# A two-block network with 64 expert evaluations on one core: four shared weight slots, a written-out TensorE order in the expert stage, second norms on transposed copies, and a ten-step root

## The chip, the cores and the metric

The kernel runs on one core of one Trainium2 chip, as one program. The time is the device time of one execution in microseconds. A core has five engines that run their own instruction streams: TensorE (PE, with its weight loads shown as PEld), VectorE (DVE), ScalarE (ACT), GpSimd (POOL) and SyncE (SP), which here issues the DMA transfers. All data are fp32. Where precision matters, a value is split into a high part rounded to the matmul format fp32r and a low part (the rest), and products are summed.

## The reference

The input is 256 tokens of width 1024. Block 1 has two layers, block 2 has two more of another kind, with 16 meta tokens put ahead of the sequence. Both blocks, cut to what matters here:

```python
for i in range(2):                                   # block 1
    mix = retention_diff_mixer(x) if i == 0 else mla_gla_mixer(x)
    x = layer_norm(ALPHA * x + mix, ln1_g[i], ln1_b[i])
    x = layer_norm(ALPHA * x + hier_moe(x), ln2_g[i], ln2_b[i])

def hier_moe(x):            # 4 groups x 8 experts; a token takes 2 experts of its best group
    # weights 1024x512 (gate), 1024x512 (up), 512x1024 (down) for each of 32 experts
    hdn = silu(xb @ w_gate[e]) * (xb @ w_up[e])
    return hdn @ w_down[e]  # then scattered back to the tokens, times the gate weight

def rms_norm(x, g):         # block 2: ahead of each layer's two halves
    return x * rsqrt(mean(x * x) + 1e-6) * g
```

In block 2 a layer is a chunked state-space mixer (SSD) beside a sliding-window attention, and then an MLP.

## The kernel before, in words

`body` (L1871) opens a pool `b1` for block 1, runs `mixer_a` (L364), the first expert stage `moe` (L667), a second norm `norm2` (L1913), `mixer_c` (L994), the second expert stage and the second norm again; it then opens pool `b2` and runs `Block2.layer` (L1435) twice.

**The weight ring.** All large weights come through a ring of slots of 128 x 2048 fp32 (1 MB each), handed out in turn by `wslot` (L144). In the expert stages `moe_ring` (L1881) has 19 entries: W and V 4 each, one S, X 4, five entries that are H tiles, and one more. The H tiles are a rotating set of `NH` = 9 (L32) that serves other data too. In an expert stage the normed tokens take three of them (`xn`, and its parts `xh` and `xl`), and the gathered tokens of four experts take one each time they are gathered, with two in use at a change. A tile is given to its new owner as soon as the last reader of the old one is done, and the load that writes it waits for that. SyncE issues loads strictly in order, so a load that waits holds up those behind it. Up to eight loads are under way at a time: load n waits also for load n-8 to have landed.

**The expert stage.** `moe` first norms the tokens (`ln_norm`, L301), routes them with small VectorE operations, and then goes over 16 pairs of experts (L921 and after). A pair has 128 slots, 64 for each expert, and the two experts' products are packed in the two column halves of TensorE's array. For each pair come twelve 1 MB loads (`load_pair`, L681: gate, up, down, each in two halves for two experts), `gate_up` (L837: 64 matmuls 128x512), on every second pair `gather` for the next four experts (L822: 32 matmuls 128x256 with one-hot matrices), `slots` (L902: two transposes of `m_PG`), `down` (L849: silu on ScalarE and VectorE, four transposes of `t2k`, ScalarE's copy `m_hT`, 32 matmuls), and `scatter` of the pair before (L874: eight matmuls on `m_pgT` and `t4k`, added to the result by VectorE). An overflow loop (L940) runs the experts that got more than 64 tokens. A list scheduler of the framework sets each engine's order from the recorded program, on TensorE too: it interleaves pieces of one pair with those of the next.

**The second norm.** `ln_stats` (L287) takes means and variances by rows, `rsqrt` (L219) takes 1/sqrt in 13 VectorE operations: an integer guess and three Newton steps. `ln_norm` writes the normed rows, half on VectorE and half on ScalarE. `norm2` then multiplies and adds gain and bias, laid out as rows over all partitions (`H<-in_ln_g`, `H<-in_ln_b`), in eight VectorE operations 128x512. After the first expert stage `to_fm` (L262) transposes the result on TensorE, in four groups of four, and `hilo` splits each group: a ScalarE cast for the high part, a VectorE subtraction for the low part. After the second stage TensorE transposes too, and the groups are copied to block 2's `h`; squares of the rows are summed on ScalarE, a small root gives each token's RMS factor, and TensorE spreads it over the partitions (`r1`). The meta tokens have a root of their own (`before_next`). In block 2 `sum_sq` (L1347), `inv_rms` (L1357) and `Block2.rsqrt` (L1366) do the same with ones-matmuls and a root on a wide tile, 128 x 272; `scaled` (L1333) applies it.

Of the kernel before, what the change touches and what calls it, by code (L numbers as in the profile page):

```python
# [125 lines left out]
class K:  # L126
# [92 lines left out]
    def rsqrt(self, v, shape, tag="rsq"):  # L219

        i = self.tl(shape, tag + "_i", 1, I32)
        y = self.tl(shape, tag + "_y", 2)
        t = self.tl(shape, tag + "_t", 1)
        hv = self.tl(shape, tag + "_h", 1)
        self.ts(i, v.bitcast(I32), 1, ALU.logical_shift_right)
        self.ts(y.bitcast(I32), i, -1.0, ALU.mult, float(0x5F3759DF), ALU.add)
        self.ts(hv, v, -0.5, ALU.mult)
# [34 lines left out]
    def to_fm(self, x_tm, f32_out=None, scale=None, bias=None):  # L262

        hi, lo = self.H(F32R), self.H(F32R)
        h = hi[:, : 8 * T].rearrange("p (k t) -> p k t", k=8)
        l = lo[:, : 8 * T].rearrange("p (k t) -> p k t", k=8)
        for j in range(4):
            ps = self.pq()
            for m in range(2):
                for i in range(2):  # L270
                    self.tr(ps[:, (2 * m + i) * P : (2 * m + i + 1) * P], x_tm[:, i, 2 * j + m :: 8])
            v = ps.rearrange("p (k t) -> p k t", k=2)
            self.hilo(h[:, 2 * j : 2 * j + 2], l[:, 2 * j : 2 * j + 2], v)
        return h, l
# [12 lines left out]
    def ln_stats(self, r, n_t=2):  # L287
# [4 lines left out]
        v = self.tl([P, 2], "ln_v", 2)  # L292
# [4 lines left out]
        self.ts(v, mv[:, :, 1], LN_EPS, ALU.add)  # L297
        y = self.rsqrt(v, [P, 2], "lnr")
# [65 lines left out]
def mixer_a(k, x_tm, moe):  # L364
# [134 lines left out]
    k.ts(ss, ss, 1.0 / 128, ALU.mult, EPS, ALU.add)  # L499
    rr = k.rsqrt(ss, [P, 2, 4], "rs8")  # L500
# [8 lines left out]
    gv = k.tl([P, 2, 4], "a_gv", 1)  # L509
# [25 lines left out]
    k.ts(gv, mv[:, :, :, 1], LN_EPS, ALU.add)  # L535
    gr = k.rsqrt(gv, [P, 2, 4], "rs8")
# [130 lines left out]
def moe(k, l, r_in, bufs, gb, rows, csb, lps, lt, then):  # L667
# [181 lines left out]
    def down(ws, g, u, gs):  # L849
# [10 lines left out]
        k.acopy(hT, tp.rearrange("p (q m) -> p q m", q=4))  # L860
        yp = [k.pd(), k.pd()]
# [78 lines left out]
    with k.tc.For_i(0, n_ov, 1) as it:  # L940
# [16 lines left out]
        pgT = k.tl([P, T], "m_pgT", 1)  # L957
# [36 lines left out]
def mixer_c(k, x_tm, xh, xl, moe):  # L994
# [243 lines left out]
    k.ts(s8, s8, 1.0 / 128, ALU.mult, EPS, ALU.add)  # L1238
    r8 = k.rsqrt(s8, [P, 8], "rs8")
# [50 lines left out]
class Block2:  # L1290
    def __init__(self, k, big, prm):

        self.k, self.big, self.prm = k, big, [prm]
# [53 lines left out]
    def sum_sq(self, h, n0, js):  # L1347

        k = self.k
        if js[0] == 0:  # L1350
            self.ss = k.pq()
# [5 lines left out]
    def inv_rms(self, n0):  # L1357

        k, ps = self.k, self.ss
        v = self.tl([P, L2], "r1", 5)  # L1360
        k.ts(v[:, n0:], ps[:, n0:L2], EPS, ALU.add)
        r = self.row()
        self.rsqrt(r[:, n0:], v[:, n0:], [P, L2 - n0])
        return r

    def rsqrt(self, y, v, shape):  # L1366
        k = self.k
        i = self.tl([P, L2], "r1", 5, I32)[: shape[0], : shape[1]]
        t = self.tl([P, L2], "r1", 5)[: shape[0], : shape[1]]
        k.ts(i, v.bitcast(I32), 1, ALU.logical_shift_right)  # L1370
        k.ts(y.bitcast(I32), i, -1.0, ALU.mult, float(0x5F3759DF), ALU.add)
        k.ts(v, v, -0.5, ALU.mult)
        for _ in range(3):
            k.mul(t, y, y)
            k.mul(t, t, v)
            k.stt(y, t, 1.5, y, ALU.add, ALU.mult)
# [58 lines left out]
    def layer(self, l, h, n0, r1=None):  # L1435
# [9 lines left out]
        if r1 is None:  # L1445
            r1 = self.inv_rms(0)
# [424 lines left out]
def body(tc, A, out):  # L1871
    from contextlib import ExitStack

    with ExitStack() as es:
# [3 lines left out]
        with tc.tile_pool(name="b1", bufs=1) as b1:  # L1878
            k.big = b1
            dense_ring = w + [("V", NV, b1, 2048)] * NV  # L1880
            moe_ring = dense_ring + [("S", 1, b1, 2048)] + [("X", NX, b1, 2048)] * NX + [("H", NH, b1, NH_F)] * 5 + [("c_phase", 1, b1, 2048)]  # L1881
# [5 lines left out]
            mt, mr = k.base.tile([P, 8, NM], F32, name="mt"), k.base.tile([NM, 1], F32, name="mr")  # L1887
            prm, rows = {}, {}

            def gain_rows(l):  # L1890

                rows[l] = k.H()[:, :2048].rearrange("p (a d) -> p a d", a=2)
                for a, n in enumerate(("ln2_g", "ln2_b")):
                    k.dma(rows[l][:, a], A[n][l : l + 1].to_broadcast([P, D]))

            def before_next():

                gain_rows(1)
# [6 lines left out]
                v = k.tl([P, 2], "ln_v", 2)[:NM, 0:1]  # L1905
                sq = k.tl([P, 1024], "t4k", NT4)[:NM]
                k.act(sq, r, AF.Square, accum_out=v)
                k.ts(v, v, 1.0 / 1024, ALU.mult, EPS, ALU.add)
                k.acopy(mr, k.rsqrt(v, [NM, 1], "lnr"))
# [3 lines left out]
            def norm2(l, r, stats=None):  # L1913

                xn, x = tm(), tm()
                k.ln_norm(xn, r)
                for c in range(2):
                    s = slice(c * 512, (c + 1) * 512)
                    for i in range(2):
                        k.mul(x[:, i, s], xn[:, i, s], rows[l][:, 0, s])  # L1920
                        k.add(x[:, i, s], x[:, i, s], rows[l][:, 1, s])
                        if stats is not None:
                            sq = k.tl([P, 512], "t2k", NT2)
                            k.act(sq, x[:, i, s], AF.Square, accum_out=stats[:, i, c : c + 1])
                return x
# [25 lines left out]
            r1 = k.pd()
            k.mm(r1[:, 0:NM], mr.to_broadcast([NM, P]), k.ident[:NM, :NM])
            for i in range(2):
                k.mm(r1[:, NM + i * P : NM + (i + 1) * P], rr[:, i : i + 1].to_broadcast([P, P]), k.ident)
        with tc.tile_pool(name="b2", bufs=1) as b2:
# [5 lines left out]
            for j in range(4):  # L1961
# [40 lines left out]
```

## Time and profile before

| | us |
|---|---|
| median of 3 runs | 2601.81 (2600.19 to 2602.08) |
| the profiled execution | 2601.37 |
| its span in the profile | 2599.6 |
| PE busy, of the span | 2422.4 (93%) |
| VectorE busy | 1391.0 (54%) |
| ScalarE busy | 1062.8 (41%) |
| expert stage 1, first gate/up product to last scatter | 174.2 to 641.5 |
| expert stage 2, the same | 854.5 to 1322.0 |
| block 2, from its first dense product | 1347.1 to the end |

Times are in us unless marked ns. In a row of the timeline stand the start, the length, the engine, the line of the code, the operation, what it writes and reads, the tile's shape and how many instructions the row joins; in brackets stands how long the engine had been idle and what it waited for. `SPq` is SyncE's queue of DMA issues: a row's length there is from its first issue to its last, so the time that the queue stands is in it. `pd` and `pq` are PSUM tiles; buffer numbers are left out.

### The profile page before, as it was taken

To read this page: it belongs to the slowest core of one execution; us is meant where nothing else is said; L and a number is where in the kernel's file an instruction comes from. 1 tells how busy PE (TensorE), PEld (TensorE's weight loads), DVE (VectorE), ACT (ScalarE), POOL (GpSimd) and SP (SyncE) were. 2 spreads that over 40 slices of the span, in tenths; PEclk is the share of its full clock that TensorE was granted. 3 is DMA by queue.
4 is the path that set the end of the run, shared out by engine and by line. 5 is a ranking of instruction groups with operands and counts; after the bars stand their busy time and mean duration, and the time that the engine had idled before them with its cause. 6 is when DMAs were issued, how large, how long until landed. Compare 5 with 4: busy or idle time off the path is not lost. (4 is left out here: it accounts for less than half of the span.)

```text
span 2599.6 us, 38742 instructions
## 1 busy us (share of the span) xinstructions
PE 2422.4 (93%) x15405; PEld 1762.8 (68%) x15405; DVE 1391.0 (54%) x2913; ACT 1062.8 (41%) x2134; POOL 8.3 (0%) x23
## 2 busy tenths in 40 slices
PE   8979999999787999999969999999998999999999
PEld 7754333334565433333338988899998898889999
DVE  6862222222576422222258878756556887866654
ACT  3421111110443211111137775655464777564654
POOL 0000000000000000000000000000000000000000
PEclk9989999999889999999979999999999999999999
DMA  8479889999634998999965542345554554335553
GB/s 299 165 296 421 367 348 421 421 402 374 237 130 168 380 385 338 421 421 421 402 223 161 179 137 98 121 162 165 173 177 132 182 173 132 114 119 179 181 187 114
DMA packets 189787, 645.16 MB, mean 248 GB/s; under 512 B 21618, under 2 KB 35988, under 8 KB 139556
## 3 DMA queue, kind: packets, MB, share of 16 engines
q1 hardware_dynamic: 189604, 642.66, 66.0%
q8 instruction: 122, 2.00, 0.3%
q14 instruction: 61, 0.50, 0.1%
HBM read 641.49 MB, written 1.12 MB: 247 GB/s over the span
## 5 line engine op out<-in xcount | busy, mean ns | idle before, releaser
L184 PE MATMUL pd<-U,Y 128*128 128x272 f32 (+1 forms) x7792 | 1011.2, 288 | 15.8 <-ACT U L193 9.2
L184 PEld LDWEIGHTS pd<-U,Y 128*128 128x128 f32 x7792 | 980.6, 189 | 30.7 <-ACT U L193 10.3
L196 DVE TENSOR_TENSOR Y<-w,Y 128x1024 fp32r<-128x1024 f32 x344 | 420.0, 1223 | 262.2 <-ACT Y L193 259.8
L184 PE MATMUL pd<-w,H 128*64 128x512 f32 (+1 forms) x2112 | 502.4, 591 | 0.9 <-DMA w<-in_moe_w_up 0.9
L193 ACT CAST Y<-w 128x1024 fp32r<-128x1024 f32 x344 | 359.7, 1047 | 330.3 <-PE pd L184 287.9
L184 PEld LDWEIGHTS pd<-w,H 128*64 128x64 f32 x2112 | 155.9, 138 | 292.3 <-issue 272.0
L184 PE MATMUL pd<-w,m_hT 128*64 128x512 f32 x1040 | 232.7, 596 | 24.4 <-ACT m_hT L193 24.4
L213 DVE SCALAR_TENSOR_TENSOR t4k<-pd,m_gs,t4k 128x512 fp32r<-128x512 f32 x64 | 48.1, 751 | 272.9 <-ACT t4k L190 270.7
L184 PEld LDWEIGHTS pd<-w,m_hT 128*64 128x64 f32 x1040 | 81.5, 137 | 152.8 <-issue 120.5
L190 ACT ACTIVATE t2k<-pd 128x512 f32<-128x512 f32 (+1 forms) x37 | 21.9, 591 | 296.1 <-PE pd L184 296.1
L190 ACT ACTIVATE t4k<-pd,m_gs 128x512 fp32r<-128x512 f32 x64 | 44.0, 687 | 210.3 <-PE pd L184 193.6
L196 DVE TENSOR_TENSOR t2k<-t2k,pd 128x512 f32<-128x512 f32 (+1 forms) x33 | 22.4, 680 | 178.2 <-PE pd L184 178.2
L196 DVE TENSOR_TENSOR H<-H,pq 128x512 f32<-128x512 f32 x132 | 84.0, 682 | 52.4 <-PE pq L184 52.2
L184 PE MATMUL pd<-Xh,H 128*128 128x512 f32 (+1 forms) x320 | 105.4, 401 | 4.1 <-ACT H L193 4.0
L193 ACT COPY m_hT<-pq 128x512 f32<-128x512 f32 (+1 forms) x34 | 19.5, 573 | 218.4 <-PE pq L187 213.5
L190 ACT ACTIVATE H<-pq,m_gb 128x256 f32<-128x256 f32 (+1 forms) x136 | 64.2, 559 | 99.3 <-PE pq L184 78.8
L213 DVE SCALAR_TENSOR_TENSOR t2k<-t2k,pd 128x512 f32<-128x512 f32 (+1 forms) x33 | 22.4, 678 | 150.6 <-ACT t2k L190 150.6
L213 DVE SCALAR_TENSOR_TENSOR r<-pd,cw,r 128x270 f32<-128x270 f32 (+1 forms) x192 | 87.8, 493 | 3.8 <-ACT r L190 2.3
L184 PEld LDWEIGHTS pq<-m_P,H 128*128 128x128 f32 x544 | 72.8, 206 | 25.0 <-issue 19.5
L184 PEld LDWEIGHTS pq<-t4k,m_pgT 128*128 128x128 f32 x256 | 43.6, 187 | 64.8 <-ACT t4k L190 20.3
L184 PE MATMUL pq<-t4k,m_pgT 128*128 128x512 f32 x256 | 80.1, 426 | 6.3 <-DVE t4k L213 6.3
L193 ACT CAST Xh<-w 128x2048 fp32r<-128x2048 f32 (+4 forms) x34 | 57.3, 1690 | 68.9 <-PE pd L184 54.5
(400 smaller groups left out, 2614.1 us busy)
## 6 DMA issues: line engine op xcount, KB each, us to landing
w<-in_moe_w_gate SPq DMA_DIRECT2D x130, 1024.0 KB, 19.8
w<-in_moe_w_down SPq DMA_DIRECT2D x130, 1024.0 KB, 19.8
w<-in_moe_w_up SPq DMA_DIRECT2D x130, 1024.0 KB, 15.9
w<-in_w_in SPq DMA_DIRECT2D x76, 1024.0 KB, 5.1
w<-in_w_mlp_up SPq DMA_DIRECT2D x32, 1024.0 KB, 5.7
w<-in_w_mlp_down SPq DMA_DIRECT2D x32, 1024.0 KB, 5.0
w<-in_w_ssd_down SPq DMA_DIRECT2D x16, 1024.0 KB, 5.8
w<-in_ev_w_in SPq DMA_DIRECT2D x14, 1024.0 KB, 13.1
```

The source lines that it names most:

```text
L184: return self.nc.tensor.matmul(out, l, r, start=start, stop=stop, **kw)
L190: return self.nc.scalar.activation(out, in_, func, **kw)
L193: return self.nc.scalar.copy(out, in_)
L196: return self.nc.vector.tensor_tensor(out=out, in0=a, in1=b, op=op)
L213: return self.nc.vector.scalar_tensor_tensor(out=out, in0=a, scalar=s, in1=b, op0=op0, op1=op1)
```

## The change

It has four parts.

**Ring.** Four of the ring's entries are H tiles instead of five, so it has 18.

**TensorE's order in the expert stage.** The loop over pairs is put under a manual schedule for TensorE: its instructions stand as the code writes them. `down` is split into `hidden` (silu, transposes, `m_hT`) and `down`, and the loop now writes gate/up, slots, gather on odd pairs, hidden, scatter of the pair before, down. The tile `m_pgT` gets two buffers instead of one. The products themselves, packed in halves, stay.

TensorE in the first expert stage, from the end of one pair's down product into the next pair, before (`w` are weight slots, the tile numbers tell pairs apart):

```order
L184 MATMUL pd_2089<-w_1966,m_hT_2086 64x512
L184 MATMUL pq_2170<-t4k_2106,m_pgT_2021 128x512
L184 MATMUL pq_2170<-t4k_2107,m_pgT_2021 128x512
L184 MATMUL pq_2174<-t4k_2106,m_pgT_2021 128x512
L184 MATMUL pq_2178<-t4k_2106,m_pgT_2021 128x512
L184 MATMUL pd_2136<-w_2112,H_2031 64x512
L184 MATMUL pq_2174<-t4k_2107,m_pgT_2021 128x512
L184 MATMUL pq_2178<-t4k_2107,m_pgT_2021 128x512
L184 MATMUL pq_2182<-t4k_2106,m_pgT_2021 128x512
L184 MATMUL pq_2182<-t4k_2107,m_pgT_2021 128x512
L187 MATMUL pq_2186<-ident,m_PG_2026 128x128 x2
```

Now, the same stage from the end of a pair's gate/up product to its down product:

```order
L184 MATMUL pd_2145<-w_2118,H_2007 64x512
L187 MATMUL pq_2162<-ident,m_PG_2002 128x128 x2
L187 MATMUL pq_2174<-ident,t2k_2170 128x128 x4
L184 MATMUL pq_2181<-t4k_2098,m_pgT_1997 128x512
L184 MATMUL pq_2181<-t4k_2099,m_pgT_1997 128x512
L184 MATMUL pq_2185<-t4k_2098,m_pgT_1997 128x512
L184 MATMUL pq_2185<-t4k_2099,m_pgT_1997 128x512
L184 MATMUL pq_2189<-t4k_2098,m_pgT_1997 128x512
L184 MATMUL pq_2189<-t4k_2099,m_pgT_1997 128x512
L184 MATMUL pq_2193<-t4k_2098,m_pgT_1997 128x512
L184 MATMUL pq_2193<-t4k_2099,m_pgT_1997 128x512
L184 MATMUL pd_2197<-w_2120,m_hT_2179 64x512
```

The scatter (`t4k`, `m_pgT`) has moved from behind its own down product, where single gate/up matmuls of the next pair stood in it, to between the next pair's hidden transposes and its down product.

**Second norms.** Gain and bias are applied to the transposed copies, where a feature is a partition, from a small tile `gc`. After the first stage `to_fm` gets it: ScalarE and VectorE each take half of a group and write it to SBUF, and `hilo` splits that. The token-major `x`, which the next mixer adds at its output, is made by four GpSimd operations 128x1024. After the second stage the gains go into the copies to `h`, the sums of squares come from `sum_sq` for the whole tile, meta tokens included, and `layer` takes `inv_rms` for its first layer too; the row squares, the two small roots and the matmuls for `r1` are gone.

VectorE at the second norm after the first stage, before: the norm (`ln_nb`, `H`), the gains, then the four low parts, read from PSUM (`pq`):

```order
L213 SCALAR_TENSOR_TENSOR ln_nb_3999<-ln_mv_3974,lnr_y_3984 128x2
L210 TENSOR_SCALAR H_3971<-H_135,lnr_y_3984,ln_nb_3999 128x1024
L196 TENSOR_TENSOR H_3972<-H_3971,H_3787 128x512 x2
L196 TENSOR_TENSOR H_3972<-H_3972,H_3787 128x512 x2
L196 TENSOR_TENSOR H_3972<-H_3971,H_3787 128x512 x2
L196 TENSOR_TENSOR H_3972<-H_3972,H_3787 128x512 x2
L196 TENSOR_TENSOR H_4012<-pq_4013,H_4011 128x512
L196 TENSOR_TENSOR H_4012<-pq_4020,H_4011 128x512
```

And now:

```order
L213 SCALAR_TENSOR_TENSOR ln_nb_3990<-ln_mv_3969,lnr_y_3977 128x2
L196 TENSOR_TENSOR Xl_4082<-w_4079,Xh_4081 128x128
L210 TENSOR_SCALAR H_3966<-H_135,lnr_y_3977,ln_nb_3990 128x1024
L210 TENSOR_SCALAR t2k_4001<-pq_3996,gc 128x256
L210 TENSOR_SCALAR t2k_4011<-pq_4006,gc 128x256
L196 TENSOR_TENSOR H_3995<-t2k_4001,H_3994 128x512
L210 TENSOR_SCALAR t2k_4021<-pq_4016,gc 128x256
L196 TENSOR_TENSOR H_3995<-t2k_4011,H_3994 128x512
```

The eight gain operations are gone from VectorE, half-width ones on the transposed groups have come in, and the low parts read two SBUF tiles.

**Root.** `root` takes ten VectorE operations instead of 13, with the small constant added inside; it serves both the narrow and the wide roots.

The diff, cut to its core:

```diff
-    def rsqrt(self, v, shape, tag="rsq"):
+    def rsqrt(self, v, shape, tag="rsq", eps=0.0):
...
-        for _ in range(3):
-            self.mul(t, y, y)
-            self.mul(t, t, hv)
-            self.stt(y, t, 1.5, y, ALU.add, ALU.mult)
+        x = self.tl(shape, tag + "_h", 1)
+        self.root(y, i, t, x, v, eps)
         return y
+    def root(self, y, i, t, x, v, eps):
+        s = 0.703952253
+        g = math.sqrt(s * 0.375)
+        self.ts(x, v, eps, ALU.add)
+        self.ts(i, x.bitcast(I32), 1, ALU.logical_shift_right)
+        self.ts(y.bitcast(I32), i, -1.0, ALU.mult, float(0x5F1FFFF9), ALU.add)
+        self.stt(t, y, -1.0, y, ALU.mult, ALU.mult)
+        self.mul(t, t, x)
+        self.stt(y, t, 2.38924456, y, ALU.add, ALU.mult)
+        self.stt(t, y, s * s * g, y, ALU.mult, ALU.mult)
+        self.mul(t, t, x)
+        self.stt(t, t, -g / 0.3, t, ALU.add, ALU.mult)
+        self.stt(y, t, 5.0 * g * g, y, ALU.add, ALU.mult)
...
-    def to_fm(self, x_tm, f32_out=None, scale=None, bias=None):
+    def to_fm(self, x_tm, gain=None):
...
+            if gain is not None:
+                y = self.tl([P, 512], "t2k", NT2).rearrange("p (k t) -> p k t", k=2)
+                g, b = (gain[:, a, 2 * j : 2 * j + 2] for a in range(2))
+                self.act(y[:, 0], v[:, 0], AF.Identity, scale=g[:, 0:1], bias=b[:, 0:1])
+                self.ts(y[:, 1], v[:, 1], g[:, 1:2], ALU.mult, b[:, 1:2], ALU.add)
+                v = y
             self.hilo(h[:, 2 * j : 2 * j + 2], l[:, 2 * j : 2 * j + 2], v)
...
-        oh, gs = k.tl([P, T], "m_pgT", 1, F32R), k.tl([P, 1], "m_gs", 2)
+        oh, gs = k.tl([P, T], "m_pgT", 2, F32R), k.tl([P, 1], "m_gs", 2)
...
-    for p in range(16):
...
-        g, u = gate_up(ws, xg, o)
-        if prev is not None:
-            scatter(*prev)
-        oh, gs = slots(pg, o)
...
-        prev = (oh, *down(ws, g, u, gs))
-    scatter(*prev)
+    with k.tc.manual_schedule(engines={mybir.EngineType.PE}):
+        for p in range(16):
...
+            g, u = gate_up(ws, xg, o)
+            oh, gs = slots(pg, o)
+            if o and q < 7:
+                pt, pg = hots(q + 1)
+                xg = gathered(pt)
+            hT = hidden(g, u)
+            if prev is not None:
+                scatter(*prev)
+            prev = (oh, *down(ws, hT, gs))
+        scatter(*prev)
...
-            moe_ring = dense_ring + [("S", 1, b1, 2048)] + [("X", NX, b1, 2048)] * NX + [("H", NH, b1, NH_F)] * 5 + [("c_phase", 1, b1, 2048)]
+            moe_ring = dense_ring + [("S", 1, b1, 2048)] + [("X", NX, b1, 2048)] * NX + [("H", NH, b1, NH_F)] * 4 + [("c_phase", 1, b1, 2048)]
...
+            def gains_0():
+                rows.append(k.H()[:, :2048].rearrange("p (a d) -> p a d", a=2))
+                for a, n in enumerate(("ln2_g", "ln2_b")):
+                    k.dma(rows[0][:, a], A[n][0:1].to_broadcast([P, D]))
+                    k.dma(gc[:, 0, a], A[n][0].rearrange("(p k) -> p k", p=P))
...
-            x = norm2(0, r)
-            xh, xl = k.to_fm(x)
+            xn, x = tm(), tm()
+            k.ln_norm(xn, r)
+            xh, xl = k.to_fm(xn, gc[:, 0])
+            for i in range(2):
+                for a, op in enumerate((ALU.mult, ALU.add)):
+                    k.nc.gpsimd.tensor_tensor(out=x[:, i], in0=(x if a else xn)[:, i], in1=rows[0][:, a], op=op)
...
+            for kk in range(8):
+                v = xps[kk // 2][:, kk % 2 * T : kk % 2 * T + T]
+                g, c = gc[:, 1, 0, kk : kk + 1], gc[:, 1, 1, kk : kk + 1]
+                if kk % 2:
+                    k.act(h[:, kk, NM:], v, AF.Identity, scale=g, bias=c)
+                else:
+                    k.ts(h[:, kk, NM:], v, g, ALU.mult, c, ALU.add)
+                b.sum_sq(h, 0, [kk])
+            b.layer(0, h, 0)
```

More of the change, by code (lines that the diff above doesn't have):

```diff
@@ L847, in gate_up, with hidden @@
         return gu
-    def down(ws, g, u, gs):
+    def hidden(g, u):
         th = k.tl([P, 512], "t2k", NT2)
@@ L860, in down @@
         k.acopy(hT, tp.rearrange("p (q m) -> p q m", q=4))
+        return hT
+    def down(ws, hT, gs):
         yp = [k.pd(), k.pd()]
@@ L1350, in sum_sq @@
         if js[0] == 0:
[L1351 removed]
+            self.ss = k.pd() if self.ss is None else k.pq()
         for j in js:
@@ L1359, in inv_rms @@
         k, ps = self.k, self.ss
-        v = self.tl([P, L2], "r1", 5)
-        k.ts(v[:, n0:], ps[:, n0:L2], EPS, ALU.add)
         r = self.row()
-        self.rsqrt(r[:, n0:], v[:, n0:], [P, L2 - n0])
+        self.rsqrt(r[:, n0:], ps[:, n0:L2], [P, L2 - n0])
         return r
     def rsqrt(self, y, v, shape):
[L1367 to L1376, printed above, removed]
+        i, t, x = (self.tl([P, L2], "r1", 5, d)[: shape[0], : shape[1]] for d in (I32, F32, F32))
+        self.k.root(y, i, t, x, v, EPS)
     def dense(self, w, cols, xh, xl, n0, evac, nk=8, pairs=False, whole=False):
@@ L1904, in before_next @@
                 k.acopy(mt, ps[:, 0:128].rearrange("p (k t) -> p k t", k=8))
[L1905 to L1909, printed above, removed]
+                r = k.tl([P, 512], "t2k", NT2)[:16, 0:P]
+                for a, n in enumerate(("ln2_g", "ln2_b")):
+                    k.dma(r[8 * a : 8 * a + 8], A[n][1].rearrange("(k p) -> k p", p=P))
+                ps = k.pq()
+                k.tr(ps[:, 0:16], r)
+                k.acopy(gc[:, 1], ps[:, 0:16].rearrange("p (a k) -> p a k", a=2))
                 w = k.tl([P, 512], "t2k", NT2)
                 prm.update(params(k, 0, k.base, [w[:, 0:P], w[:, P : 2 * P]]))
[L1913 to L1925, printed above, removed]
             k.set_ring(moe_ring)
-            r = moe.run(r, bufs, lambda: gain_rows(0))
+            r = moe.run(r, bufs, gains_0)
             k.set_ring(dense_ring)
-            x = norm2(0, r)
-            xh, xl = k.to_fm(x)
+            xn, x = tm(), tm()
[4 more added lines that the diff above has]
+                    k.nc.gpsimd.tensor_tensor(out=x[:, i], in0=(x if a else xn)[:, i], in1=rows[0][:, a], op=op)
             moe = Moe(k, 1)
@@ L1947, in body @@
                         kk = 2 * j + m
-                        k.tr(ps[:, (2 * m + i) * P : (2 * m + i + 1) * P], x[:, i, kk * P : (kk + 1) * P])
+                        k.tr(ps[:, (2 * m + i) * P : (2 * m + i + 1) * P], xn[:, i, kk * P : (kk + 1) * P])
                 xps.append(ps)
[L1951 to L1954, printed above, removed]
         with tc.tile_pool(name="b2", bufs=1) as b2:
```

69 lines of the change are left out of this document (21 added, 48 removed).

## The prediction

> **What bounds the kernel now.** I read the table by stage first (where time is spent, whether TensorE or the transfers fill it), then the DMA queue's waits and SyncE's rows (why the transfers pause), then TensorE's rows. Windows: start and end, length, busy time of PE, PEld, DVE, ACT, POOL, then granted clock, DMA share, GB/s.
>
> ```profile
> 262.00:278.00 16.00, 14.40 (x69) 6.32 (x68) 2.14 (x4) 4.07 (x8) 0.00 (x0) 1.00 0.63 245
> 320.00:340.00 20.00, 18.40 (x90) 7.78 (x91) 2.13 (x4) 4.84 (x10) 0.00 (x0) 1.00 0.38 144
> 340.00:560.00 220.00, 207.12 (x921) 83.74 (x918) 51.74 (x92) 30.85 (x54) 0.00 (x0) 1.00 1.01 422
> 560.00:580.00 20.00, 18.40 (x90) 7.78 (x91) 1.37 (x2) 4.83 (x10) 0.00 (x0) 1.00 0.89 360
> 930.00:960.00 30.00, 28.40 (x130) 12.16 (x127) 7.64 (x14) 6.26 (x12) 0.00 (x0) 1.00 0.84 342
> 1000.00:1022.00 22.00, 20.40 (x99) 8.57 (x100) 2.13 (x4) 4.83 (x10) 0.00 (x0) 1.00 0.44 172
> 1240.00:1260.00 20.00, 18.40 (x91) 7.94 (x92) 1.37 (x2) 4.83 (x10) 0.00 (x0) 1.00 0.88 355
> ```
>
> In both expert stages the transfers run at 422 GB/s, and a load of 1,024 KB takes 2.485 us, the 12 loads of a pair of experts 29.8 us. There are three holes a stage. Each is worth its length times the missing part of 422: 6.7 + 13.2 + 2.9 = 22.8 us in the first stage, 5.7 + 13.0 + 3.2 = 21.9 in the second. In each hole SyncE's queue stands before one load, which issues as TensorE ends the gate and up product of an odd pair (267.04 + 7.08 = 274.12, and 323.75 + 10.51 = 334.26; the third is alike):
>
> ```profile
> 274.18 0.33 SPq L181 DMA_DIRECT2D w<-in_moe_w_up  x1
> 334.64 0.33 SPq L181 DMA_DIRECT2D w<-in_moe_w_gate  x1
> 267.04 7.08 PE L184 MATMUL pd<-w,H 128*64 128x512 f32 x30
> 323.75 10.51 PE L184 MATMUL pd<-w,H 128*64 128x512 f32 x46
> ```
>
> That product is the last reader of the gathered tokens, which sit in the H tiles, among them the ring's five weight slots. Three H tiles are held by the token arrays, two are wanted by gathered tokens, five by weights: ten for nine. So a load inherits the tile of the gathered tokens.
>
> Yet TensorE hardly waits for a load. These are its waits from 345 to 620 (total, times, longest), and two places near the stage's end, the first of them its first wait for a load:
>
> ```profile
> PE pq L187 <- DVE t2k L196: 7.4, 9, 0.9
> PE pd L184 <- ACT m_hT L193: 6.6, 9, 0.7
> PE pq L184 <- DVE t4k L213: 2.3, 8, 0.3
> 625.27 3.65 PE L184 MATMUL pd<-w,H 128*64 128x512 f32 x14 [0.38 <-DMA w<-in_moe_w_up]
> 639.62 1.88 PE L184 MATMUL pq<-t4k,m_pgT 128*128 128x512 f32 x7 [0.29 <-DVE t4k L213]
> ```
>
> So two bounds lie side by side: TensorE in program order, and the transfers with holes; they meet at the end. Only a change that moves both shortens the stage, and it then ends with the later of the two.
>
> **The expert stage.** TensorE's pieces where they stand whole (the gather is one of the second stage; brackets are idle time before the row), and the load with which the queue starts again:
>
> ```profile
> 177.91 0.33 SPq L181 DMA_DIRECT2D w<-in_moe_w_up  x1
> 174.23 13.95 PE L184 MATMUL pd<-w,H 128*64 128x512 f32 x64
> 893.52 4.01 PE L184 MATMUL pq<-m_P,H 128*128 128x256 f32 x32
> 190.43 7.09 PE L184 MATMUL pd<-w,m_hT 128*64 128x512 f32 x32 [0.68 <-ACT m_hT L193]
> 211.18 2.08 PE L184 MATMUL pq<-t4k,m_pgT 128*128 128x512 f32 x8
> 514.98 0.72 PE L187 MATMUL pq<-ident,t2k 128*128 128x128 f32 x4 [0.87 <-DVE t2k L196]
> 575.13 0.72 PE L187 MATMUL pq<-ident,t2k 128*128 128x128 f32 x4 [0.87 <-DVE t2k L196]
> ```
>
> Two pairs now take 575.13 - 514.98 = 60.15 us, 30.1 a pair. The pieces are gate/up 13.95, the two slot transposes (half of the four hidden ones, 0.36), the hidden transposes 0.72, scatter 2.08 and down 7.09, in sum 24.2, and the gather's 4.0 more on odd pairs: 26.2 on average. The fixed order puts the slot transposes, and on odd pairs the gather, between gate/up and the hidden transposes, so the 0.87 us wait for VectorE becomes about 0.5 on even pairs and none on odd ones. Scatter (2.08) stands between the hidden transposes and the down product, over the copy m_hT, for which TensorE waits 0.7 now. The 0.28 us wait for t4k goes, since the scatter is a whole gate/up later than its data. I take 26.5 us a pair. With nothing to wait for, TensorE would end near 174.2 + 16 x 26.5 + 2.1 = 600.
>
> With four H slots weights and gathered tokens fit (3 + 2 + 4 = 9), so the holes go. The ring holds 18 loads instead of 19, so one load more is moved within the stage: 2.5 us. The first stage's last scatter ends at 639.62 + 1.88 = 641.5 now, behind loads for which TensorE has begun to wait (625.27). Without holes those loads, and with them the end, come 22.8 - 2.5 = 20.3 us earlier, the scatter near 621; TensorE's 600 is below that, so the loads decide, and TensorE has slack until 27.8 us a pair. A new hole would need a load's slot (freed by the 18th load before it) to come free later than the queue reaches it. The tightest is the down product of the first odd pair, now behind gather, hidden and scatter: its first slots come free near 197.5 + 13.9 + 0.4 + 4.0 + 0.7 + 2.1 + 3.6 = 222, and the queue, full again from about 178 (177.91), reaches that load at 178 + 20 x 2.485 = 227.7. Later margins grow by 3 us a pair. The second stage has the same order: 21.9 - 2.5 = 19.4. Together **-39.7 us**. Bounds: -8.8 if TensorE needs 28.8 us a pair (first rival), -44.7 if the two extra loads hide.
>
> **Second norm after the first expert stage.**
>
> ```profile
> 682.01 3.78 PE L187 MATMUL pq<-ident,H 128*128 128x128 f32 x16 [13.37 <-DVE H L196]
> 676.81 0.81 DVE L210 TENSOR_SCALAR H<-H,lnr_y,ln_nb 128x1024 f32<-128x1024 f32 x1
> 677.65 4.91 DVE L196 TENSOR_TENSOR H<-H,H 128x512 f32<-128x512 f32 x8
> 676.81 1.24 ACT L190 ACTIVATE H<-H,ln_nb,lnr_y 128x1024 f32<-128x1024 f32 x1 [2.28 <-DVE ln_nb L213]
> 683.56 1.23 ACT L193 CAST H<-pq 128x512 fp32r<-128x512 f32 x2 [5.51 <-PE pq L187]
> ```
>
> The eight multiplies and adds (4.91) leave the path: transposes can start near 678.1 instead of 682.0, 3.9 earlier. Each of the four groups now gets a gain ahead of its cast, half of it on ScalarE and half on VectorE; by the cast's length (0.62 for twice the elements) that is at most 2.5 on ScalarE, a third of it under the transposes: 3.9 - 1.7 = **-2.2** (-3.9 to -1.4). GpSimd gets the four 128x1024 multiplies and adds of x, needed only at the mixer's output; nothing waits for them unless they block VectorE (rival).
>
> **Roots.** A small root loses 3 of 13 operations. What waits for a first norm, two neighbouring steps of a small root, and a wide root (128x272) with what it ends in:
>
> ```profile
> 847.03 0.61 PE L184 MATMUL pq<-m_sel,m_lt 128*128 128x64 f32 x2 [10.37 <-DVE m_sc L216]
> 676.41 0.16 DVE L213 SCALAR_TENSOR_TENSOR lnr_y<-lnr_t,lnr_y 128x2 f32<-128x2 f32 x1
> 676.61 0.16 DVE L213 SCALAR_TENSOR_TENSOR ln_nb<-ln_mv,lnr_y 128x2 f32<-128x2 f32 x1
> 1985.55 0.44 DVE L209 TENSOR_SCALAR r<-pq 128x272 f32<-128x272 f32 x1 [1.34 <-PE pq L184]
> 1991.07 1.33 DVE L213 SCALAR_TENSOR_TENSOR r<-U,pb,row 128x272 f32<-128x272 f32 x3
> 1992.07 1.32 PE L184 MATMUL pd<-U,Y 128*128 128x272 f32 x4 [6.57 <-ACT U L193]
> ```
>
> Dependent small operations start 0.20 apart, so a root on the path gains 0.6: two first norms (TensorE idle 10.37 there) -1.2, the second norm above -0.6. The mixers' roots I put at -1.0 (0 to -2.4). The wide root before the second layer of block 2 is on the path: 1991.07 - 1985.55 = 5.5 us for 13 operations; three fewer at the mean of 0.42 make -1.2, and leave 4.3. The other wide roots run under dense products: -0.5. Sum **-4.5**.
>
> **Into block 2.** The path loses the eight multiplies and adds (4.91 on VectorE), the 16x1 root, a small root and its products. It gains four gains and eight squares on ScalarE (half-width operations: at most 12 x 0.62 = 7.4 by the cast above, part of it under the transposes), eight products with ones, and a ten-step wide root (4.3) ahead of the first scaling.
>
> ```profile
> 1347.13 1.30 PE L184 MATMUL pd<-U,Y 128*128 128x272 f32 x4 [2.67 <-ACT U L193]
> 1353.17 7.07 PE L184 MATMUL pd<-U,Y 128*128 128x272 f32 x37 [2.25 <-ACT Y L193]
> ```
>
> Today the dense product starts at 1347.13 but runs steadily only from 1353.17. What is dropped and what is added differ by less than that 6 us of slow start, so I take **0** (-3 to +5).
>
> **Sum.** -39.7 - 2.2 - 4.5 = -46.4. The profiled execution took 2601.4 (span 2599.6 and 1.8 around it), the median is 2601.8: 2601.8 - 46.4 = **2555.4 us**.
>
> **Rivals.** *TensorE stays the bound.* If PSUM tiles or VectorE's queue, now met in a fixed order, cost 2.3 us a pair, it runs at 28.8: 174.2 + 460.8 + 2.1 = 637, 4.4 earlier than now, twice: 2601.8 - 8.8 - 6.7 = 2586. For: the pieces above stood whole only in the first pairs. Against: none of TensorE's waits in the list above exceeds 0.9 us.
>
> *GpSimd holds VectorE up at the second norm.* These are GpSimd's nearest rows:
>
> ```profile
> 670.70 1.04 POOL L1007 CAST m_lt<-t4k 128x1024 uint8<-128x1024 f32 x1 [34.91 <-DVE H L196]
> 702.54 2.01 POOL L1157 COPY H<-phase 32x1024 f32<-32x1024 f32 x1 [30.81 <-DVE phase L196]
> ```
>
> Four operations of 1 to 2 us: if VectorE's low-part subtractions (now with both inputs in SBUF) each wait for one, +4 to +8; with +8 the time is 2563. No row settles it: beside the 702.54 copy VectorE had started first. The Trainium skill, "SBUF — State Buffer", section "Who interferes with whom", says that a VectorE instruction with two SBUF inputs contends with a GpSimd instruction that reads SBUF, and that whoever issues second fully blocks; that rule speaks for this rival.
>
> *The change doesn't do what it says*: tokens and weights still collide, the holes stay, and only the norms and roots gain: 2601.8 - 6.7 = 2595.
>
> *Slower: the clock.* Waiting for loads, TensorE would idle some 3.3 us a pair in pieces of 1 to 1.5. After a 1.85 us gap the granted clock was 0.73:
>
> ```profile
> 640.00:650.00 10.00, 7.76 (x41) 6.95 (x39) 3.89 (x12) 0.71 (x3) 0.00 (x0) 0.73 0.70 252
> 643.35 1.84 PE L184 MATMUL pq<-m_P,H 128*128 128x64 f32 x13 [1.85 <-DVE m_P L196]
> ```
>
> At 0.80 a pair takes 26.2 / 0.80 + 0.3 = 33.1, 3.3 over the loads: 32 x 3.3 - 46.4 = +59, 2661. It decides from 0.89 down, and turns the sign from 0.84. Against: a TensorE that is late no longer waits, so the clock returns; and 1.00 was granted with 0.9 us waits in every pair. The Trainium skill, "TensorE: Matmul & The Clock Gate", section "Part 1: The HAM clock gate", asks for an idle window of about 3.4 us; the 0.73 after a 1.85 us gap is lower than that rule gives.
>
> **The numbers.** Forecast 0.55 (2548 to 2562 by its unknown terms), GpSimd 0.17, TensorE bound 0.14, no change in the holes 0.07 (two thirds of it over 0.2%, 5.2 us, about what a measurement can tell), clock 0.05, better than 2548 0.02. Faster: 0.55 + 0.17 + 0.14 + 0.045 + 0.02 = 0.92, same 0.03, slower 0.05. The TensorE case begins at 27.8 us a pair without a loss, so 2580 takes in some six tenths of it; the range from 2547 to 2580 leaves out the rest of it, the holes, the clock and the gain beyond: 0.06 + 0.07 + 0.05 + 0.02 = 2 in 10.
>
> **What would show it.** Right: SyncE's rows without a pause over 10 us in either stage, 421 GB/s throughout, waits of TensorE for loads in every pair, the last scatter near 621, transposes of the second norm near 682.0 - 20.3 - 4.5 = 657.2. Wrong: TensorE's waits for VectorE or ScalarE inside a pair above 1.3 us, a granted clock below 0.89 in the stage, VectorE's subtractions of the second norm 1 us apart or more while GpSimd works, or last scatter after 630.

## The result

The changed kernel takes 2564.5 us (2559.8 to 2567.4, four runs) against 2601.5 before; the ratio is 0.9857, with a 95% interval from 0.9839 to 0.9874. That is 37 us less, where 46 were forecast (2555.4), and within the range. The profiled execution of the changed kernel took 2567.4 us at a span of 2565.5, so it lies at the slow end of its runs; against the span of before it is 34.1 us shorter. By places of the two traces:

| stretch | before | after | difference | forecast |
|---|---|---|---|---|
| to the first gate/up product | 174.2 | 172.7 | -1.5 | -1.1 |
| expert stage 1, to its last scatter | 467.3 | 451.4 | -15.9 | -20.3 |
| from there to ScalarE's first table load in the second mixer | 51.7 | 54.7 | +3.1 | -2.8 |
| from there to the next gate/up product | 161.3 | 159.1 | -2.2 | -1.1 |
| expert stage 2 | 467.5 | 450.7 | -16.8 | -19.4 |
| from there to block 2's first table load | 63.5 | 63.5 | 0 | 0 |
| the rest | 1214.1 | 1213.3 | -0.8 | -1.7 |

The table loads serve as marks only; both kernels have them at the same places of the program. The forecast of the roots, -4.5, is spread over the rows where they stand.

### The expert stages

The table by stage of the changed kernel, with the columns of the prediction's table, has no hole left. Shown are the times where before had its holes in the first stage, and the largest of the second's:

```profile
262.00:278.00 16.00, 16.00 (x89) 8.26 (x90) 5.86 (x12) 5.60 (x11) 0.00 (x0) 1.00 1.01 420
320.00:340.00 20.00, 20.00 (x92) 6.49 (x88) 2.19 (x3) 1.97 (x3) 0.00 (x0) 1.00 1.02 420
340.00:560.00 220.00, 196.66 (x928) 81.46 (x928) 50.94 (x91) 33.05 (x61) 0.00 (x0) 1.00 1.01 421
560.00:580.00 20.00, 18.55 (x85) 6.01 (x82) 2.19 (x3) 1.97 (x3) 0.00 (x0) 1.00 1.01 420
1000.00:1022.00 22.00, 20.23 (x92) 8.36 (x90) 5.33 (x9) 1.96 (x3) 0.00 (x0) 1.00 1.01 420
```

TensorE's waits from 345 to 600 have changed hands. Before, all were for VectorE and ScalarE inside a pair. Now most are for loads:

```profile
PE pd L184 <- DMA w<-in_moe_w_up: 15.9, 12, 1.3
PE pd L184 <- DMA w<-in_moe_w_gate: 8.1, 5, 2.9
PE pq L187 <- DVE t2k L196: 1.6, 4, 0.4
```

TensorE's own pace can be read where it does not yet wait for loads, which is up to 355. These are the slot transposes of two odd pairs, four pairs apart:

```profile
209.64 0.44 PE L187 MATMUL pq<-ident,m_PG 128*128 128x128 f32 x2
312.27 0.44 PE L187 MATMUL pq<-ident,m_PG 128*128 128x128 f32 x2
```

That is 102.6 us for four pairs, 25.7 a pair, against 30.1 before and 29.8 for a pair's loads. The granted clock stays at 1.00 in this stage, with waits of up to 2.9 us in it, so the rival of the clock fell. The Trainium skill, "TensorE: Matmul & The Clock Gate", section "Part 1: The HAM clock gate", wants an idle window of about 3.4 us before the clock drops; these waits agree with it. Other waits here don't: the kernel with five H slots and x on VectorE (below) waits 2.41 us for a load up to 412.93, and from 414 to 418 its granted clock is 0.57. So a wait under 3.4 us came with a lower clock there, and the measurement decides.

The end of the first stage in TensorE's timeline:

```profile
607.03 3.65 PE L184 MATMUL pd<-w,H 128*64 128x512 f32 x14 [1.34 <-DMA w<-in_moe_w_up]
610.61 0.44 PE L187 MATMUL pq<-ident,m_PG 128*128 128x128 f32 x2
611.46 0.75 PE L187 MATMUL pq<-ident,t2k 128*128 128x128 f32 x4 [0.41 <-DVE t2k L196]
614.00 7.09 PE L184 MATMUL pd<-w,m_hT 128*64 128x512 f32 x32
621.85 2.25 PE L184 MATMUL pq<-t4k,m_pgT 128*128 128x512 f32 x7 [0.28 <-DVE t4k L213]
```

The last wait for an up weight ends at 607.03, against 625.27 before: 18.2 us earlier. From there to the last scatter it takes 17.07 us instead of 16.23, with the scatter of the pair before now in this tail. In SyncE's rows one load issues 4.02 us after its predecessor instead of 2.49:

```profile
413.97 0.33 SPq L181 DMA_DIRECT2D w<-in_moe_w_down  x1
```

```profile
417.99 0.33 SPq L181 DMA_DIRECT2D w<-in_moe_w_down  x1
```

A stage that is bound by transfers passes such a delay on.

### The second norm after the first stage

TensorE's transposes, GpSimd's four operations and VectorE's rows behind them, from the changed kernel:

```profile
660.85 3.68 PE L187 MATMUL pq<-ident,H 128*128 128x128 f32 x16 [9.38 <-ACT H L190]
668.92 0.42 PE L184 MATMUL pd<-H,Xh 128*32 128x256 f32 x1 [1.88 <-DVE H L196]
671.70 0.42 PE L184 MATMUL pd<-H,Xh 128*32 128x256 f32 x1 [1.29 <-DVE H L196]
```

```profile
660.88 10.21 POOL L1928 TENSOR_TENSOR H<-H,H 128x1024 f32<-128x1024 f32 x4 [6.32 <-ACT H L190]
```

```profile
663.97 2.13 DVE L196 TENSOR_TENSOR H<-t2k,H 128x512 fp32r<-128x512 f32 x1
666.02 0.53 DVE L210 TENSOR_SCALAR t2k<-pq,gc 128x256 f32<-128x256 f32 x1
666.48 2.39 DVE L196 TENSOR_TENSOR H<-t2k,H 128x512 fp32r<-128x512 f32 x1
668.79 0.53 DVE L210 TENSOR_SCALAR t2k<-pq,gc 128x256 f32<-128x256 f32 x1
669.25 3.00 DVE L196 TENSOR_TENSOR H<-t2k,H 128x512 fp32r<-128x512 f32 x2
```

The idle time before the transposes fell from 13.37 to 9.38 us, by 4.0 as forecast. Then the low-part subtractions take 2.13 and 2.39 us each while GpSimd is at work, and the dense product waits for them three times. In the kernel before two of them, with one input in PSUM, took 1.33 together:

```profile
684.18 1.33 DVE L196 TENSOR_TENSOR H<-pq,H 128x512 fp32r<-128x512 f32 x2 [1.62 <-ACT H L193]
```

Behind these waits TensorE's granted clock is low too, 0.57 from 668 to 676 (last three columns: clock, DMA share, GB/s):

```profile
668.00:676.00 8.00, 5.79 (x27) 4.35 (x27) 6.25 (x6) 3.19 (x4) 3.10 (x2) 0.57 0.30 90
```

### Into block 2

```profile
1298.99 3.68 PE L187 MATMUL pq<-ident,H 128*128 128x128 f32 x16 [7.37 <-ACT H L190]
1304.47 7.02 PE L184 MATMUL pd<-r,k 128*128 128x272 f32 x16 [1.80 <-ACT r L190]
1319.03 26.16 PE L184 MATMUL pd<-U,Y 128*128 128x272 f32 x187 [7.22 <-ACT U L193]
```

The dense products start late, at 1319.03, but run steadily from there, 30.3 us behind the last scatter (1288.7) where it was 31.2: what went and what came cancel. The wide root before the second layer of block 2 lasts from 1950.76 to 1955.31, 4.6 us instead of 5.5, and TensorE waits 5.59 there instead of 6.57:

```profile
1956.32 8.94 PE L184 MATMUL pd<-U,Y 128*128 128x272 f32 x46 [5.59 <-ACT U L193]
```

### The profile page after: what moved, and what is told of

The parts are those of the page before. It is cut to its first block, busy times and chain, and to the rows that moved or that the text cites. A ratio compares the mean times of both kernels' runs of the same rounds, so it can differ in the third digit from the quotient of the medians.

```text
span 2565.5 us, 38758 instructions
## 1 busy us (share of the span) xinstructions
PE 2383.6 (93%) x15416; PEld 1748.8 (68%) x15416; DVE 1379.7 (54%) x2844; ACT 1062.1 (41%) x2138; POOL 18.5 (1%) x27
## 4 chain that ended last, share of the span: by engine, by line
PE 53%; DMA 13%; DVE 5%; ACT 3%; issue 1%; ACTq 0%; SPq 0%; DVEq 0%
PE pd L184 44%; PE pq L184 7%; DMA w<-in_moe_w_up 5%; DMA w<-in_moe_w_down 5%; DMA w<-in_moe_w_gate 3%; PE pq L187 2%; DVE Y L196 1%; ACT Y L193 1%; DVE r L213 0%; ACT cb L190 0%; DVE H L196 0%; ACT r L190 0%; DVE cb L209 0%; DVE Xl L196 0%; DVE sg L209 0%
## 5 line engine op out<-in xcount | busy, mean ns | idle before, releaser
L184 PE MATMUL pd<-w,H 128*64 128x512 f32 (+1 forms) x2112 | 483.9, 592 | 53.6 <-DMA w<-in_moe_w_up 37.8
L184 PEld LDWEIGHTS pd<-w,H 128*64 128x64 f32 x2112 | 159.1, 138 | 371.7 <-issue 257.1
L184 PEld LDWEIGHTS pd<-w,m_hT 128*64 128x64 f32 x1040 | 71.6, 137 | 143.0 <-issue 139.0
L184 PE MATMUL pd<-Z,Y 128*128 128x272 f32 (+1 forms) x512 | 84.2, 286 | 0.0
L196 DVE TENSOR_TENSOR Xl<-w,Xh 128x2048 fp32r<-128x2048 f32 (+4 forms) x34 | 69.0, 2033 | 27.0 <-ACT Xh L193 26.8
L184 PE MATMUL pd<-H,Xh 128*128 128x256 f32 (+1 forms) x352 | 68.7, 296 | 7.0 <-DVE H L196 4.6
```

Source lines behind the costliest of these rows:

```text
L184: return self.nc.tensor.matmul(out, l, r, start=start, stop=stop, **kw)
L196: return self.nc.vector.tensor_tensor(out=out, in0=a, in1=b, op=op)
```

## The experiments

Theory at this point: the stages are now bound by transfers, and the second norm loses to GpSimd what it gained. Open: whether the ring or the order closed the holes, what the roots are worth, and whether VectorE and GpSimd really shut each other out. Kernels of one group ran on the same chip beside the kernel before, whose median was 2599.5 to 2600.5 in the groups; ratios are to it. The changed kernel's own ratio, 0.9857, is to 2601.5, so a comparison with it by ratios can differ from one by medians by 1 or 2 us.

### Ring or order

Four H slots alone, on the kernel before:

```diff
- ... + [("H", NH, b1, NH_F)] * 5 + ...
+ ... + [("H", NH, b1, NH_F)] * 4 + ...
```

> The kernel before with four H slots in the ring instead of five, and nothing else. Theory 1, as in the prediction (two bounds side by side): TensorE keeps its 30 us a pair and waits for loads no more than now, so the holes go but the time stays within 5 us of before, 2597 to 2603. Theory 2 (the holes are the bound): they are worth 20 us a stage, so 2560 to 2570.

Measured: 2594.2 us, ratio 0.9977 (0.9967 to 0.9986). The table by stage and TensorE's waits from 345 to 600:

```profile
320.00:340.00 20.00, 18.40 (x90) 7.56 (x92) 2.13 (x4) 4.82 (x10) 0.00 (x0) 1.00 1.01 420
```

```profile
PE pq L187 <- DVE t2k L196: 6.6, 8, 0.9
PE pd L184 <- ACT m_hT L193: 5.8, 8, 0.7
PE pq L184 <- DVE t4k L213: 2.0, 7, 0.3
```

The hole is gone (420 GB/s where there were 144), and TensorE's busy time in the stretch is the same 18.40, its waits the same. The stages shrink by 1.3 and 1.9 us. Theory 1 holds for the stages; the time is 2.8 us under its range. Of the 6 us, 2.4 lie between the stages (210.6 us from the first stage's last scatter to the next gate/up product, against 213.0, one profile each); they are not explained.

The order alone, with five H slots:

```diff
-    for p in range(16):
-        ... gate_up, scatter(prev), slots, gather, down(ws, g, u, gs)
+    with k.tc.manual_schedule(engines={mybir.EngineType.PE}):
+        for p in range(16):
+            ... gate_up, slots, gather, hidden(g, u), scatter(prev), down(ws, hT, gs)
```

> The kernel before with the fixed TensorE order in the expert stage (and two m_pgT buffers), still five H slots. Theory 1, as in the prediction (both are needed): loads still wait for the gathered tokens' tile, holes of about half the old length stay, 2580 to 2590. Theory 2 (the holes are the bound): over 2590. Theory 3 (the order alone does it: the holes were the shadow of a late TensorE, and close when an odd pair's gate/up product ends 7 us earlier at the first and 17 us earlier at the second): the whole gain of the stage, 2563 to 2572, with at most one hole of 3 us a stage.

Measured: 2560.8 us, ratio 0.9847 (0.9830 to 0.9863): the whole gain and no less, 2 us under the range of theory 3. No hole is left here either:

```profile
262.00:278.00 16.00, 16.00 (x90) 8.41 (x90) 5.90 (x12) 5.67 (x11) 0.00 (x0) 1.00 1.02 421
320.00:340.00 20.00, 20.00 (x96) 6.58 (x92) 2.56 (x4) 1.97 (x3) 0.00 (x0) 1.00 1.01 422
```

```profile
PE pd L184 <- DMA w<-in_moe_w_up: 14.6, 11, 1.4
PE pd L184 <- DMA w<-in_moe_w_gate: 6.2, 4, 2.3
```

Theory 3 holds. The holes were the shadow of a late TensorE: the load that inherits the gathered tokens' tile still waits for the odd pair's gate/up product, but that product now ends before the eight loads under way run out. At the second hole that load issues 15.7 us after the one before it (297.16 and 312.85), where it was 29.4 in the kernel before (305.26 and 334.64); eight loads of 2.49 last 19.9. The second buffer of `m_pgT` came with the order; the two weren't run apart.

Both, with the old norms and roots:

> The kernel before with both, ring of four and fixed order, but the old norms and the old root. After changed the two stages by -15.9 and -16.8 us by the traces, so 2565 to 2572 by all theories, if norms and root together are worth as little as the traces say (-1 to -4 us net); if norms and root were worth the predicted -6.7, 2571 to 2575.

Measured: 2561.5 us, ratio 0.9850 (0.9833 to 0.9866), 3.5 under the expected range. The profiles have stages of 449.4 and 450.5 us, against 446.3 and 448.2 with five slots: the fourfold ring costs 3.1 and 2.3 us, about the one load of 2.5 that the prediction had, and brings nothing once the order is fixed. The medians, 0.7 apart, can't tell the two. And this kernel without the new norms and roots is no slower than the changed kernel with them (0.9857).

### Bound by transfers or by TensorE

One more 1 MB load at the end of every second pair's loads, eight a stage, on each of the two kernels; nobody reads it:

```diff
                 out[j][n // 2].append(ld(v, kk // 2, v.shape[2]))
+        if es[0] % 4 == 2:
+            ld(v, kk // 2, v.shape[2])
         return out
```

> The changed kernel with one more 1 MB load at the end of every second pair's loads, read by nobody: 8 a stage, 19.9 us of transfer at 2.485 each. Theory 1 (the stage is bound by transfers now): the stages grow by nearly all of it, 15 to 20 us each, 2595 to 2605. Theory 2 (TensorE in its fixed order is still the bound and its waits for loads are slack): within 8 us of 2564.

Measured: 2601.5 us, ratio 1.0008 (0.9999 to 1.0018): 37 us more than the changed kernel by medians and 39 by ratios, for 39.8 us of transfer. The stages last 469.0 and 467.3 us.

> The same additional loads in the kernel before. Theory 1 (TensorE bound, the holes being idle time of the transfers): 19.9 us fit into holes of 22.8 and 21.9 a stage, so 2600 to 2610. Theory 2 (the holes are the bound): the loads come on top, 2630 to 2640.

Measured: 2611.4 us, ratio 1.0043 (1.0027 to 1.0058): 12 us more than before, for the same 39.8, and 1.4 over the range of theory 1. TensorE's waits from 172 to 645, in the changed kernel with the loads and in the kernel before with them:

```profile
PE pd L184 <- DMA w<-in_moe_w_up: 28.3, 22, 1.3
PE pd L184 <- DMA w<-in_moe_w_gate: 13.4, 10, 2.9
```

```profile
PE pd L184 <- ACT m_hT L193: 13.7, 16, 2.5
PE pq L187 <- DVE t2k L196: 10.4, 13, 0.9
PE pq L184 <- DVE t4k L213: 3.4, 12, 0.3
PE pd L184 <- DMA w<-in_moe_w_up: 3.1, 4, 1.3
```

Theory 1 holds for both: the stage was TensorE's, with transfers close behind, and is the transfers' now. An additional load also takes a slot of the ring; but in the changed kernel with them the transfers run on at 421 GB/s from 262 to 560 and from 880 to 1290, so there it is the transfers that cost the time.

### The root

The changed kernel with 13 operations a root:

```diff
+        self.ts(x, x, -0.5, ALU.mult)
+        for _ in range(3):
+            self.mul(t, y, y)
+            self.mul(t, t, x)
+            self.stt(y, t, 1.5, y, ALU.add, ALU.mult)
```

> The changed kernel with 13 operations in each root again (same inputs, eps inside, three Newton steps). The prediction put the roots at -4.5 us, so 2568 to 2570 beside 2564.5. By the traces of the two kernels the roots gave about 0.6 at each of the narrow ones on the path and 0.8 in all of block 2, so +3 to +4. Rival: roots are under other work and it stays within 1.5 us of the changed kernel.

Measured: 2569.5 us, ratio 0.9881 (0.9864 to 0.9897), 5 us over the changed kernel by medians, 2.0 by the spans of the two profiled runs. The sign is as predicted, but the intervals overlap (0.9874 and 0.9864), so the size is no better known than 2 to 6. From the second stage's last scatter to the end the two profiles differ by 0.2 (1276.6 with 13 operations, 1276.8 with ten): no gain shows in block 2 as a whole.

### GpSimd against VectorE

First, the four operations of x held back until the last low part is done, by a true dependence:

```diff
+            g0 = rows[0][:, 0, 0:1]
+            k.stt(g0, xl[:, 7, T - 1 : T], 0.0, g0, ALU.mult, ALU.add)
             for i in range(2):
                 ... gpsimd.tensor_tensor(out=x[:, i], ...)
```

> The changed kernel, in which the four GpSimd operations of x wait for the last low part of the second norm: a one-column VectorE operation behind it rewrites one column of the gain rows with its own value. Theory 1 (GpSimd and VectorE shut each other out while both read two SBUF tiles): the four low-part subtractions take 0.7 us each again instead of 2.1 to 2.4, and the dense products behind them start 5 to 6 us earlier; the next two-input subtractions, 128x1152, now meet GpSimd instead, so 2 to 6 us less in all: 2558 to 2562. Theory 2 (the subtractions are slow for another reason, such as the place of their operands): they stay at 2.1 to 2.4, 2564.

Measured: 2563.7 us, ratio 0.9854 (0.9839 to 0.9869), as the changed kernel and 2 over the range of theory 1. VectorE and GpSimd:

```profile
665.96 0.68 DVE L196 TENSOR_TENSOR H<-t2k,H 128x512 fp32r<-128x512 f32 x1
666.56 0.54 DVE L210 TENSOR_SCALAR t2k<-pq,gc 128x256 f32<-128x256 f32 x1
667.02 1.46 DVE L196 TENSOR_TENSOR H<-t2k,H 128x512 fp32r<-128x512 f32 x2
668.84 6.99 DVE L196 TENSOR_TENSOR Xl<-w,Xh 128x1152 fp32r<-128x1152 f32 x2 [0.17 <-ACT Xh L193]
```

```profile
668.82 11.58 POOL L1930 TENSOR_TENSOR H<-H,H 128x1024 f32<-128x1024 f32 x4 [12.43 <-ACT Xh L193]
```

The same subtractions are back at 0.68 to 0.73 us, and the next two-input ones, 128x1152, take 3.5 us each instead of 1.35: the cost moved with GpSimd. Theory 1 of the mechanism holds; the hoped-for gain doesn't come, since the weights' low parts stand before the dense product just as the tokens' do: TensorE waits 2.45 us for one of them (`Xl`) at 672.5.

Second, x on VectorE:

```diff
-                    k.nc.gpsimd.tensor_tensor(out=x[:, i], ...)
+                    k.nc.vector.tensor_tensor(out=x[:, i], ...)
```

> The changed kernel with the four operations of x on VectorE instead of GpSimd; the scheduler puts them among the low parts and behind them. Theory 1 (lock): the subtractions take 0.7 us each, the four operations 1.2 us each, one of them ahead of the last low part, so the dense products start 4 to 5 us earlier, and the rest of the 4.9 us delays later subtractions: 2559 to 2563. Theory 2 (another reason): subtractions at 2.1 to 2.4 and 4.9 us more on VectorE, 2565 to 2569.

Measured: 2558.4 us, ratio 0.9838 (0.9823 to 0.9853), 6 us under the changed kernel by medians and 5 by ratios, though the intervals overlap. The subtractions take 0.68 and the four operations 1.2 each, and the granted clock from 668 to 676 is 1.00:

```profile
667.07 0.68 DVE L196 TENSOR_TENSOR H<-t2k,H 128x512 fp32r<-128x512 f32 x1
667.67 0.54 DVE L210 TENSOR_SCALAR t2k<-pq,gc 128x256 f32<-128x256 f32 x1
668.12 0.68 DVE L196 TENSOR_TENSOR H<-t2k,H 128x512 fp32r<-128x512 f32 x1
668.72 1.22 DVE L1928 TENSOR_TENSOR H<-H,H 128x1024 f32<-128x1024 f32 x1
```

```profile
668.00:676.00 8.00, 6.90 (x43) 4.56 (x42) 8.00 (x10) 4.97 (x8) 0.00 (x0) 1.00 0.51 166
```

The traces tell the two placements apart more surely than the times. From the first stage's last scatter to the next gate/up product the five profiled kernels with x on GpSimd take 213.9 to 216.9 us, the three with x on VectorE (two of them below) 209.2 to 210.5, and the six with the old norm 210.6 to 213.4. So 4.9 us of work on the engine that is waited for cost less than 10.2 us on the other one; part of the price is the low clock behind the waits. The Trainium skill, "SBUF — State Buffer", section "Who interferes with whom", has the rule, an exclusive lock on the shared port pair; all three traces agree with it: 2.13 to 2.39 us beside GpSimd, 0.68 to 0.73 without.

### Combinations

The kernel before with the fixed order and a ten-step root, and the old second norms:

> The kernel before with the fixed TensorE order and the ten-step root (nine operations and the old addition of eps); five H slots, old second norms. The order alone gave 2560.8, and taking the ten-step root out of the changed kernel cost 2 us by the traces and 5 by the medians, so 2555 to 2559 if the second norms on transposed copies cost more than they bring, which puts it below the changed kernel; 2561 or more if the root does nothing.

Measured: 2558.5 us, ratio 0.9839 (0.9826 to 0.9852), in the range for new second norms that, with x on GpSimd, cost more than they bring; the interval overlaps that of the changed kernel. Its profile has 1272.4 us from the second stage's last scatter to the end, against 1276.4 with the order alone and 1275.0 to 1276.8 in all eight kernels with the new norms. By these profiles the ten-step root gained 4 us there with the old way into block 2, and the new way may give them back; that rests on one profile, and the runs don't show where.

The changed kernel with five H slots and late x:

> The changed kernel with five H slots again and the late x of the run before. Five slots: the stages begin with one load more in the ring and end 2 to 3.5 us earlier each, as in the run with the order alone; late x: 2 to 6 us. 2551 to 2558. If four slots were of use, no faster than late x alone.

Measured: 2559.8 us, ratio 0.9842 (0.9828 to 0.9855), 2 us over the range.

The changed kernel with five H slots and x on VectorE:

> The changed kernel with five H slots and with x on VectorE. Late x gave nothing (the delay moved to the next subtractions), x on VectorE gave 6; five slots should give 1 to 3 us a stage: 2553 to 2557. If five slots are of no use: 2558.

Measured: 2556.1 us (2553.2 to 2557.9), ratio 0.9832 (0.9819 to 0.9846). It has the lowest median of all kernels here, 8 us under the changed kernel (6.5 by ratios); the two intervals overlap by 0.0007. It is 2 under the kernel with the fixed order, the ten-step root and the old norms (2558.5), which is within the scatter.

The same, with the scatter of the pair before between gate and up:

```diff
         for m in range(2):
+            if m and mid is not None:
+                scatter(*mid)
             ps = k.pd()
```

> As the run before it, and the scatter of the pair before between the gate and the up product. In a stage bound by transfers the scatter then runs while TensorE waits for the up weights, and 2.1 us less stand behind the last load of a stage, less the 0.7 us wait for m_hT that shows again: 2550 to 2555, 1 to 3 us under it. If TensorE is the bound, 10 us more, as the 0.7 us wait returns in every pair.

Measured: 2559.1 us, ratio 0.9846 (0.9833 to 0.9860), 3 over its sister (the intervals overlap) and 4 over the range, so my expectation failed. One of the three holes of before is back in each stage; here are the window, the second half of an odd pair's gate/up product, and SyncE's rows, in which the third gate load comes only with the end of that product, at 319.58 (in the sister the product ends at 312.3):

```profile
314.00:322.00 8.00, 8.00 (x49) 4.15 (x46) 2.21 (x6) 1.17 (x3) 0.00 (x0) 1.00 0.30 97
```

```profile
312.41 7.09 PE L184 MATMUL pd<-w,H 128*64 128x512 f32 x32
```

```profile
294.52 25.87 SPq L181 DMA_DIRECT2D w<-in_moe_w_gate  x4
320.44 2.55 SPq L181 DMA_DIRECT2D w<-in_moe_w_up  x4
```

With the scatter inside it the gate/up product ends at 319.5, 7 us later, and the queue stands 22.3 us (from 297.29) where it stood 14.6 in the sister; the loads under way have run out at 314. So five slots stand near an edge: the fourfold ring would be insurance at about 2.5 us a stage against a TensorE that is a few us late.

## Why the prediction was right, and where it was not

**What bounds the stage.** That TensorE and the transfers lie side by side, and that the transfers take over, was right: 39.8 us of additional transfers cost 12 before and 37 after. The step that failed is "Only a change that moves both shortens the stage": the order alone gave the whole gain (2560.8), the ring alone 6 us. The prediction took the holes for a cause; they were idle time of the transfers behind a late TensorE. It had the number for this at hand, the load that issues when the odd product ends, and did not ask where that end goes when TensorE gains 3 us a pair. As the change had both parts, this step left the sum untouched; that the time fell in the range says nothing for it.

**The term of the stages.** -39.7 us forecast, -32.7 in the traces. The 2.5 us for one load less were about right (3.1 and 2.3 by the pair of runs above). In the second stage 2.6 are missing: 0.8 in the tail, since the scatter stands in it, and 1.9 in the loads, of which the 140 issued from 911.85 to 1261.68 come 2.499 us apart, where the sum took 2.485. In the first stage 4.4 are missing: 0.8 in the same tail and 1.9 in the 142 loads from 242.30 to 597.09, most of it the one that came 1.5 us late; of the other 1.7 the runs don't show the cause. The same order and ring with the old norms took 2.0 less there (449.4), so part of it may be scatter between executions. TensorE's 26.5 us a pair were close: it takes 25.7 as long as it doesn't wait for loads.

**The second norm.** The transposes came 4.0 us earlier as worked out, 0.6 of it the root's. The forecast of -2.2 for what follows failed: from the stage's end to the mark in the mixer it is +3.1. What decided was the rival that had 0.17, GpSimd holding up VectorE, priced at +4 to +8 and at 2563 for the whole kernel. One of the prediction's signs of being wrong came with it: subtractions that start 2.5 us apart (663.97 and 666.48) while GpSimd works. The price was about right: the profiles with x on GpSimd and on VectorE lie 3.4 to 7.7 us apart between the stages. It held no term for TensorE's clock, which fell to 0.57 behind the waits. The likeliest case should have been this one: the only row at hand, the copy, could not speak against it, as the prediction itself said, and the rule that it quoted from the Trainium skill spoke for it.

**Roots and block 2.** The roots' -4.5 lies within 2 to 6 us, but the runs don't bear it out part by part. The wide one gave 1.0 of the 1.2 forecast in its own rows, yet nothing shows in block 2 as a whole. The way into block 2 gave nothing up to the first table load, as forecast (and may have cost up to 4 by the run with the old way), but not for the reason of a slow start: the wide root there takes from 1311.5 to 1318.0, as two weight subtractions of 1.2 us stand in it on VectorE.

**The other rivals.** TensorE stays the bound, the clock, and a change that leaves the holes all fell.

## What to carry to other kernels

A pause of the transfers is a cause only if somebody waits for the transfers behind it; read who waits at the end of the stage, and ask what the pause becomes when the engine it waits for gets faster. When two bounds lie side by side, add work to one and see whether the time moves: this told more than any row. When times scatter as widely as the effect, compare one stretch over all traces. In this kernel work moved to GpSimd wasn't free while VectorE read two SBUF tiles beside it; four operations there cost more than the same four on the busy VectorE.

## What the runs showed of the hardware beyond that

Four GpSimd operations of 128x1024 took 10.2 and 11.6 us beside VectorE, 2.6 to 2.9 each, against 1.2 each on VectorE. Executions of the kernels that transfers bound scatter more: 2559.8 to 2567.4 for the changed kernel, against 2600.2 to 2602.1 for the one before (whether the transfers are the cause was not tested), so that a difference of 2 us between two of the faster kernels needs more runs than were made here.
